# Input projection of a two-layer RWKV-7 and attention block: the work between its matmuls as queued steps, weights split a column ahead

## The chip, the cores and the metric

The kernel runs on one core of one Trainium2 chip. The metric is device time in microseconds (us) of one execution; less is better.

## What is computed

Two layers, each a token mixer and a convolutional feed-forward block, on 1024 latent and 256 context tokens of width 1024. The change touches the mixer's input projection. Cut to what matters there:

```python
mod_lat = silu(c) @ w_ada[l] + b_ada[l]          # shift, scale, gate; 6 x 1024
p = u @ w_in[l]                                  # u = x * (1 + sc1) + sh1
r, k, v, w_lo, a_lo, g_lo = split(dwconv3(p[..., :RWKV_COLS], rwkv_conv))
w_log = -softplus(-(w0 + tanh(w_lo) @ w_b)) - 0.5     # per direction
decay = exp(-exp(w_log)); a = sigmoid(a0 + a_lo @ a_b)
g = sigmoid(g_lo) @ g_b
kk = k * k_k; kk = kk / max(sqrt(sum(kk * kk)), 1e-12)    # per head of 64
k_dir = k * (1 + (a - 1) * k_a)
q = rms_norm(c_q, q_norm_g) @ w_uq; kv = rms_norm(c_kv, kv_norm_g) @ w_ukv
```

Layer 1 (the last) needs r, the queries and the gate for latent tokens only; layer 0 for all 1280.

## The kernel before

Everything is held with features on the 128 partitions and tokens along the free axis, in float32. A matmul in float32 precision is made of three fast ones: weights and inputs are split into a high and a low part (`split_w`, L259: a DMA into `raw`, a copy `whi` on ACT, a difference `wlo` on DVE), and `project` (L275, matmul in L284) adds high x high, high x low and low x high into one PSUM tile.

`in_proj` (L300) makes the projection column by column of 128 features; a column of 1280 tokens is 72 matmuls (48 of 512 tokens, 24 of 256), a latent one 48. It has two PSUM tiles for columns (tag pj) and two small ones (tag sm). Its first part makes keys and queries of the attention: columns 18 and 19 (`latent`, L327), 20, the products with w_uk and w_uv, columns 15 to 17, and `queries` (L408). Each latent's sums of squares go through a root on POOL (rs, L352) and a broadcast (`along`, L355) before its products can be scaled.

The second part makes the operands of the recurrence. `column` (L483) makes one column, and the depthwise convolution `conv` (L286) reads it from PSUM: ACT writes the middle tap (L291), DVE adds the two others (L295, L298). Columns 12 and 13 come first: inputs `lw` and `la` of the low-rank products. Then, for each of four head pairs: `key` (L501; the norm kk by block sums, L498, with Ln and Exp on ACT), `value` (L512; v less its mean, and transposes L526), r, and for each direction `operands` (L543), which takes the rank products (`lora`, L532, matmuls L538, tanh L540 on ACT), scans the decay (L550), takes exponentials E (L551, L552) and multiplies kx, rx, the keys and the rates. Direction 1 of a pair and its `bonus` come one column later, in the next pair's place. Column 14 and `gates` (L441) close the stage.

In layer 0, 40 modulations (`modulation`, L160; two weight tiles wt of 512 KB by DMA, sums L172, an evacuation ev on DVE, products L187 or L181) are spread over the 15 columns from 12 on (L488).

A scheduler (`schedule_with_timeline_sim=True`) turns the program into one queue for each engine; an engine takes its queue in order. DMAs that load weights are issued from SP's queue. A weight split is written in the program just before its column's matmuls, from a pool of 3 tiles a tag.

Of the kernel before, what the change touches and what calls it, by code (L numbers as in the profile page):

```python
# [16 lines left out]
NLAT = 1024  # L17
# [48 lines left out]
NT = 13  # L66
# [14 lines left out]
class Kern:  # L81
# [78 lines left out]
    def modulation(self, l, ch, wtile=None, pj=None):  # L160

        nc, a, M = self.nc, self.a, self.M
        cols = slice(ch * 256, (ch + 1) * 256)
        wt = []
        for k4 in range(2):
            w = (wtile or self.mod_tile)()
            nc.sync.dma_start(out=w, in_=a["w_ada"][l, ch, :, 4 * k4:4 * k4 + 4])
            wt.append(w)
        ps = M.pp.tile([128, 512], F32, name="ps", tag="sm")
        for k in range(8):  # L170
            r = 32 * (k % 4)
            nc.tensor.matmul(ps[r:r + 32, :256], M.sc[:, k, :], wt[k // 4][:, k % 4, :], start=k < 4, stop=k >= 4)  # L172
        ev = M.p.tile([128, 256], F32, name="ev", tag="ev", bufs=2)
        nc.vector.tensor_copy(ev, ps[:, :256])
        sel = self.cst[:, CO_SEL:CO_SEL + 2]
        s = ch // 4
        pt = pj.tile([128, 1536], F32, name="pt", tag="pj") if pj else M.pp.tile([128, 512], F32, name="pt", tag="sm")
        if s in (2, 5):
            mt = M.p.tile([2, 256], F32, name="mt", tag="mt", bufs=2)
            nc.sync.dma_start(out=mt, in_=a["b_ada"][l:l + 1, cols].to_broadcast([2, 256]))  # L180
            nc.tensor.matmul(pt[0:2, :256], sel, ev, start=True, stop=True)  # L181
            nc.vector.tensor_tensor(mt, pt[0:2, :256], mt, op=ALU.add)
            nc.sync.dma_start(out=self.mods[l].rearrange("r s d -> r (s d)")[:, cols], in_=mt)
            return

        for i in range(2):
            nc.tensor.matmul(pt[:, 2 * i:2 * i + 2], ev[:, i * 128:(i + 1) * 128], sel, start=True, stop=True)  # L187
        k = 2 * (ch % 4)
        dst = self.msc[l][:, s - s // 3, :, k:k + 2]
        b = bc(self.pv[l][:, None, PV_BA + 2 * ch:PV_BA + 2 * ch + 2], [128, 2, 2])  # L190
        nc.vector.scalar_tensor_tensor(dst, pt[:, 0:4].rearrange("p (k r) -> p r k", r=2), float(s in (1, 4)), b,
                                       op0=ALU.add, op1=ALU.add)
# [38 lines left out]
    def first_u(self, p, pp, pj):  # L231
# [17 lines left out]
        for i, ch in enumerate((0, 4, 1, 5, 2, 6, 3, 7)):  # L249
            self.modulation(0, ch, lambda: spare.pop(0)(), pj)  # L250
# [8 lines left out]
    def split_w(self, src, n, p):  # L259
# [3 lines left out]
        for o in range(0, n, 512):  # L263
            m = min(512, n - o)
            raw = p.tile([128, 512], F32, name="raw", tag="raw")
# [34 lines left out]
    def in_proj(self, l, up):  # L300
        tc, nc, a = self.tc, self.nc, self.a
        need_ctx = l < DEPTH - 1
        pv = self.pv[l]
        with ExitStack() as st:
# [3 lines left out]
            todo = []  # L308
            if l == 0:
                self.alloc_u(up)  # L310
                self.mod_setup(st, 2, sm)
                todo = [(0, ch) for ch in range(8, 24)] + [(1, ch) for ch in range(24)]

            def col(j, segs):
                w = self.split_w(a["w_in"][l, j], D, wp)
# [4 lines left out]
            with tc.tile_pool(name=f"iq{l}", bufs=1, reuse_waits="tile") as p:  # L320
# [3 lines left out]
                if l == 0:  # L324
                    self.first_u(p, sm, pj)

# [1001 lines left out]
```

## Time and profile before

| | us |
|---|---|
| median of 3 runs | 4700.81 (4693.97 to 4705.19) |
| profiled execution | 4693.84 |
| its span | 4692.1 |
| mean granted TensorE clock | 0.928 |
| PE, DVE, ACT, POOL busy | 4161.5, 2733.6, 1679.0, 548.8 |

The profile is of one execution. Engines: PE is TensorE's matmuls, PEld its weight loads, DVE VectorE, ACT ScalarE, POOL GpSimd, SP SyncE. A busy time counts instructions at work; matmuls are pipelined, so PE's busy time is partly overlap. PEclk is the granted clock as a share of full speed. A row of a wait names who waited, at which line, for whose result at which line.

In this execution layer 0's projection stage lies at 42 to 752 us and layer 1's at 2549 to 3136. The convolutions of the four key columns start at 309.92, 401.99, 506.15 and 611.72 us, and at 2771.38, 2833.96, 2927.88 and 3022.35. The first attention matmuls start at 751.91 and 3136.22.

### The profile page before, as it was taken

The page shows a single profiled execution, that of the slowest core. Times are in us where ns is not written, and L with a number is a line of the kernel's source. Part 1 is how long each engine was busy: PE and PEld are TensorE (multiplying, and loading weights), DVE is VectorE, ACT ScalarE, POOL GpSimd, SP SyncE. Part 2 cuts the span into 40 slices and gives each one's busy share as a digit, 9 for nine tenths or more (in the row PEclk, how much of TensorE's full clock was granted, in tenths as well). Part 3 has the DMA queues.
Part 4 walks back from the last instruction along what each step waited for, and adds up shares of the span by engine and source line. Part 5 has one row for each costly group of instructions (what it writes and reads, how often), then busy time and mean ns, then how long its engine had stood idle before and what let it go on. Part 6 is the DMA issues. An engine that isn't in the chain of part 4 may idle for free. (4 is left out here: it accounts for less than half of the span.)

```text
span 4692.1 us, 72915 instructions
## 1 busy us (share of the span) xinstructions
PE 4161.5 (89%) x29598; PEld 3295.4 (70%) x29598; DVE 2733.6 (58%) x4939; ACT 1679.0 (36%) x2996; POOL 548.8 (12%) x498
## 2 busy tenths in 40 slices
PE   7987777888988899999998987768889878999998
PEld 6865545777766688888886764446777656888887
DVE  3234446888885635445446224468888857555556
ACT  3213334454554432212224224354444544222222
POOL 1000000111222300000004000001111224100002
PEclk9988887999998999999998998869898989999999
DMA  4334554222323311111112222242222333111111
GB/s 170 109 132 146 163 181 144 72 71 72 88 72 124 101 36 37 45 32 39 43 39 99 85 74 97 81 143 69 65 74 74 74 117 132 61 50 45 45 52 66
DMA packets 425697, 401.36 MB, mean 86 GB/s; under 512 B 243472, under 2 KB 329936, under 8 KB 425360
## 3 DMA queue, kind: packets, MB, share of 16 engines
q1 hardware_dynamic: 425360, 396.69, 27.4%
q8 instruction: 233, 3.82, 0.3%
q14 instruction: 104, 0.85, 0.1%
HBM read 285.85 MB, written 110.72 MB: 85 GB/s over the span
## 5 line engine op out<-in xcount | busy, mean ns | idle before, releaser
L1139 PE MATMUL up<-u,hi 128*128 128x512 f32 (+1 forms) x3520 | 1012.9, 369 | 5.8 <-ACT hi L1130 5.8
L1139 PEld LDWEIGHTS up<-u,hi 128*128 128x128 f32 x3520 | 643.7, 189 | 121.4 <-ACT hi L1130 6.5
L1139 PE MATMUL up<-u,lo 128*128 128x512 f32 (+1 forms) x1760 | 648.8, 369 | 0.2
L284 PE MATMUL pj<-u,whi 128*128 128x512 f32 (+1 forms) x1888 | 567.1, 385 | 62.4 <-DVE o L298 35.3
L1186 DVE TENSOR_TENSOR acc<-dn,acc 128x512 f32<-128x512 f32 x340 | 233.4, 689 | 432.2 <-PE dn L1180 432.1
L284 PEld LDWEIGHTS pj<-u,whi 128*128 128x128 f32 x1888 | 351.2, 198 | 162.5 <-issue 58.4
L284 PE MATMUL pj<-u,wlo 128*128 128x512 f32 (+1 forms) x944 | 357.2, 379 | 22.1 <-DVE wlo L270 22.1
L1139 PEld LDWEIGHTS up<-u,lo 128*128 128x128 f32 x1760 | 332.4, 189 | 59.1 <-DVE lo L1132 1.5
L945 PE MATMUL sp<-ka,qa 96*128 96x512 f32 (+1 forms) x1200 | 315.0, 395 | 30.9 <-ACT P L958 21.5
L1180 PE MATMUL dn<-hi,fh 128*128 128x512 f32 x792 | 311.3, 393 | 8.2 <-DVE acc L1186 4.0
L1130 ACT ACTIVATE hi<-raw 128x512 fp32r<-128x512 f32 x176 | 110.3, 630 | 566.7 <-PE up L1139 563.3
L1180 PE MATMUL dn<-lo,fh 128*128 128x512 f32 x792 | 309.8, 391 | 0.0
L1180 PE MATMUL dn<-hi,fl 128*128 128x512 f32 x792 | 305.8, 390 | 0.0
L958 ACT ACTIVATE P<-sp,mx 128x512 f32<-128x512 f32 (+1 forms) x400 | 239.8, 606 | 178.4 <-DVE mx L955 125.6
L987 PE MATMUL av<-pT,va 128*64 128x128 f32 x2624 | 235.1, 303 | 52.2 <-DVE pT L982 28.2
L945 PEld LDWEIGHTS sp<-ka,qa 96*128 96x128 f32 x1200 | 213.6, 203 | 79.4 <-ACT P L958 29.8
L946 DVE TENSOR_REDUCE mx<-sp 128x1 f32<-128x512 f32 (+1 forms) x400 | 228.3, 586 | 43.1 <-PE sp L945 40.6
L270 DVE TENSOR_TENSOR wlo<-raw,whi 128x512 fp32r<-128x512 f32 (+2 forms) x110 | 71.5, 654 | 294.0 <-ACT whi L268 288.8
L977 PE MATMUL tp<-cst,P 128*128 128x128 f32 x1312 | 234.1, 301 | 5.7 <-ACT P L958 2.6
L284 PEld LDWEIGHTS pj<-u,wlo 128*128 128x128 f32 x944 | 185.4, 196 | 63.9 <-DVE wlo L270 25.4
L987 PEld LDWEIGHTS av<-pT,va 128*64 128x64 f32 x2624 | 153.4, 147 | 107.3 <-DVE pT L982 34.6
L1132 DVE TENSOR_TENSOR lo<-raw,hi 128x512 fp32r<-128x512 f32 x176 | 125.2, 714 | 175.8 <-ACT hi L1130 163.4
(254 smaller groups left out, 7227.2 us busy)
## 6 DMA issues: line engine op xcount, KB each, us to landing
wt<-in_w_ada_dram SPq DMA_DIRECT2D x96, 512.0 KB
raw<-in_w_up_dram SPq DMA_DIRECT2D x176, 256.0 KB
raw<-in_w_down_dram SPq DMA_DIRECT2D x88, 256.0 KB
raw<-in_w_in_dram SPq DMA_DIRECT2D x84, 256.0 KB
bkD<-lt SPq DMA_DIRECT2D x32, 640.0 KB
BK<-bkD SPq DMA_DIRECT2D x320, 64.0 KB
KR<-kkD SPq DMA_DIRECT2D x152, 128.0 KB
vtD<-vt SPq DMA_DIRECT2D x16, 640.0 KB
```

The lines of the kernel that those rows point to most:

```text
L270: nc.vector.tensor_tensor(lo[:, :m], raw[:, :m], hi[:, :m], op=ALU.subtract)
L284: nc.tensor.matmul(ps[:, o:o + n], ww, u[k][s], start=k == 0 and j == 0, stop=k == nk - 1 and j == 2)
L945: nc.tensor.matmul(sp[:, o - b0:o - b0 + n], q[:, qq, e], A.k[e][:, kk, o:o + n], start=m == 0, stop=m == 2)
L946: nc.vector.tensor_reduce(mx[:, i:i + 1], sp[:, :w], axis=AX.X, op=ALU.min)
L958: nc.scalar.activation(P[:, o:o + w], sp[:, :w], AF.Exp, bias=mn, scale=-1.0, accum_out=mx[:, 4 + i:5 + i])
L977: nc.tensor.transpose(tp[:, b, e], Ps[e][:, o:o + 128], self.ident)
L987: nc.tensor.matmul(av[half[e], 0:128], A.v[:, k0 // 128 + kt, half[e]], pT[:, b, e], start=kt == 0, stop=kt == nkt - 1)
L1130: nc.scalar.activation(hi, raw, AF.Copy)
L1132: nc.vector.tensor_tensor(lo, raw, hi, op=ALU.subtract)
L1139: nc.tensor.matmul(ps[:, so:so + sn], ww, uu[k][s], start=k == 0 and m == 0, stop=k == 7 and m == 2)
L1180: nc.tensor.matmul(ps, x[:, t * 128:(t + 1) * 128], w, start=m == 0, stop=m == 3 * len(js) - 1)
L1186: nc.vector.tensor_tensor(dst, ps, dst, op=ALU.add)
```

## The change

- `project` runs queued steps: after every 4 of its 8 k-tiles it pops an even share of `self.queue`.
- A list `ws` holds the weights in the order of use, and `weights()` splits one further ahead before it hands one out; pools of 4 (raw 3).
- `modulation` returns loads, sums and results. All 40 are queued in the keys' and queries' part, 8 steps a column or product.
- Columns 12 and 13 stand between the queries' latents and their products; latent sums and the root are steps.
- In a pair the columns come as k, r, v (in the last pair 14 ahead of v), and `key`, `value`, `ranks`, `operands`, `bonus` and `bonus2` return lists of steps that are woven and run within the next columns. The last pair's rest goes between the gate's four products.
- Two rope products move from POOL to DVE, the gate's scale from POOL to ACT. Temporary tiles: 12 of tag t and 5 of tag s in place of 13.

```diff
-NT = 13
+NT = 12
+NS = 5
...
+        wt, evs = [], []
+        def loads():
+            for k4 in range(2):
+                w = (wtile or self.mod_tile)()
+                nc.sync.dma_start(out=w, in_=a["w_ada"][l, ch, :, 4 * k4:4 * k4 + 4])
+                wt.append(w)
+        def sums():
+            ps = M.pp.tile([128, 512], F32, name="ps", tag="sm")
+            for k in range(8):
+                r = 32 * (k % 4)
+                nc.tensor.matmul(ps[r:r + 32, :256], M.sc[:, k, :], wt[k // 4][:, k % 4, :], start=k < 4, stop=k >= 4)
+            ev = M.p.tile([128, 256], F32, name="ev", tag="ev", bufs=2)
+            nc.vector.tensor_copy(ev, ps[:, :256])
+            evs.append(ev)
...
+        def results():
+            ev = evs[0]
...
+        return loads, sums, results
...
-            raw = p.tile([128, 512], F32, name="raw", tag="raw")
+            raw = p.tile([128, 512], F32, name="raw", tag="raw", bufs=3)
...
+        gaps = sum(-(-nk // 4) if SEGS[s][1] > 256 else 1 for s in segs)
         for s in segs:
             o, n = SEGS[s]
             for k in range(nk):
                 wh, wl = [x[:, (k % 4) * 128:(k % 4 + 1) * 128] for x in w[k // 4]]
                 for j, (ww, u) in enumerate(((wh, uh), (wh, ul), (wl, uh))):
                     nc.tensor.matmul(ps[:, o:o + n], ww, u[k][s], start=k == 0 and j == 0, stop=k == nk - 1 and j == 2)
+                if k == nk - 1 or (k % 4 == 3 and n > 256):
+                    self.between(-(-len(self.queue) // gaps))
+                    gaps -= 1
+    def between(self, n):
+        for _ in range(min(n, len(self.queue))):
+            self.queue.pop(0)()
...
-            wp = st.enter_context(tc.tile_pool(name=f"iw{l}", bufs=3, side="right", reuse_waits="tile"))
+            wp = st.enter_context(tc.tile_pool(name=f"iw{l}", bufs=4, side="right", reuse_waits="tile"))
...
+            ws = [a["w_in"][l, j] for j in (18, 19, 20)] + [a["w_uk"][l, j] for j in range(NP)] + [a["w_uv"][l]]
+            ws += [a["w_in"][l, j] for j in (15, 16, 17, 12, 13)] + [a["w_uq"][l, j] for j in range(6)]
+            for q in range(NP):
+                ws += [a["w_in"][l, j] for j in ([4 + q, q, 14, 8 + q] if q == NP - 1 else [4 + q, q, 8 + q])]
+            ws.append(a["g_b"][l])
+            ahead = []
+            def weights():
+                for _ in range(2 - len(ahead)):
+                    if ws:
+                        w = ws.pop(0)
+                        ahead.append(self.split_w(w, w.shape[-1], wp))
+                return ahead.pop(0)
...
+                todo = [(0, ch) for ch in range(8, 24)] + [(1, ch) for ch in range(24)] if l == 0 else []
+                mods = [self.modulation(*m) for m in todo]
+                steps = [m[0] for m in mods[:2]]
+                for i, m in enumerate(mods):
+                    steps += [m[1]] + [x[0] for x in mods[i + 2:i + 3]] + [m[2]]
+                share = -(-len(steps) // 17)
+                def some():
+                    queue.extend(steps[:share])
+                    del steps[:share]
...
+                        def sums(i=i, sq=sq):
+                            ssp = sm.tile([128, 512], F32, name="ssp", tag="sm")
+                            for t in range(nt):
+                                nc.tensor.matmul(ssp[:, t:t + 1], sq[:, t * 128:(t + 1) * 128], self.cst[:, CO_ONE:CO_ONE + 1],
+                                                 start=True, stop=True)
+                            if i:
+                                nc.vector.tensor_tensor(ss[:, :nt], ss[:, :nt], ssp[:, :nt], op=ALU.add)
+                            else:
+                                nc.vector.tensor_copy(ss[:, :nt], ssp[:, :nt])
...
+                for j, (x, f) in enumerate(((lw, AF.Tanh), (la, AF.Copy))):
+                    some()
+                    ps = col(ALL)
+                    o = tmp("o")
+                    self.conv(o, ps, PV_CONV + 3 * (12 + j), pv, True)
+                    nc.scalar.activation(x, o, f)
+                rb = along(rs, nr, -QK_SCALE)
...
+                short = name in ("kx", "rx", "oc", "ocr", "vt")
+                return p.tile([128, NTOK], dt, name=name, tag="s" if short else "t", bufs=NS if short else NT)
...
+                ss = blocks(sq, NTOK, lambda ps, s: nc.vector.tensor_scalar(sq[:, s], ps, 1e-24, None, op0=ALU.max))
+                return ss + [lambda: nc.scalar.activation(sq, sq, AF.Ln),
+                             lambda: nc.scalar.activation(sq, sq, AF.Exp, scale=-0.5),
+                             lambda: nc.vector.scalar_tensor_tensor(sq, o, kcol, sq, op0=ALU.mult, op1=ALU.mult)]
...
+                return out[:3] + [lambda: scan(0)] + out[3:5] + [lambda: scan(NTOK // 2)] + out[5:] + [decay, keys]
...
+                return [kx, rx, lambda: stt(ta, ta, 1.0, rv(kk), op0=ALU.add, op1=ALU.mult), b2,
+                        lambda: tt(kd, kd, rv(k), op=ALU.mult), k2]
...
+            def weave(x, y):
+                r = [((i + 0.5) / len(v), j, f) for j, v in enumerate((x, y)) for i, f in enumerate(v)]
+                return [f for _, _, f in sorted(r, key=lambda e: e[:2])]
...
+            old = ps = None
+            for q in range(NP):
+                c = {}
+                if old:
+                    old["v"] = convolved(8 + q - 1, ps, True)
+                    queue += weave(operands(old, q - 1, 1) + bonus(old, q - 1), value(old, q - 1))
                 else:
-                    og = column(14, need_ctx)
-                if old:
-                    q0, k0, kk0, v0, r0, kd0 = old
-                    kb = bonus(q0, [kd0, operands(q0, 1, k0, kk0, r0)], r0, v0)
-                if q == NP:
-                    gates(og, nr)
-                    bonus2(q0, kb, v0)
-                    break
-                v = value(q)
-                if old:
-                    bonus2(q0, kb, v0)
-                r = column(q, need_ctx)
-                old = q, k, kk, v, r, operands(q, 0, k, kk, r)
+                    queue += ranks(c, q, 0)
+                ps = col(ALL)
+                c["k"] = convolved(4 + q, ps, True)
+                queue += weave(bonus2(old, q - 1) + ranks(c, q, 0), key(c, q)) if old else key(c, q)
+                ps = col(segs)
+                c["r"] = convolved(q, ps, need_ctx)
+                queue += weave(operands(c, q, 0), ranks(c, q, 1))
+                if q == NP - 1:
+                    ps = col(segs)
+                    og = convolved(14, ps, need_ctx)
+                    nc.scalar.activation(og, og, AF.Tanh, scale=0.5)
+                    nc.scalar.activation(og, og, AF.Copy, scale=0.5, bias=0.5)
+                    gh, gl = tmp("gh", F32R)[:, :nr], tmp("gl", F32R)[:, :nr]
+                    nc.scalar.activation(gh, og, AF.Copy)
+                    nc.vector.tensor_tensor(gl, og, gh, op=ALU.subtract)
+                ps = col(ALL)
+                old = c
+            old["v"] = convolved(8 + NP - 1, ps, True)
+            rest = weave(operands(old, q, 1) + bonus(old, q), value(old, q)) + bonus2(old, q)
+            w = weights()
+            parts = [[[x[:, so:so + sn] for so, sn in SEGS[:len(segs)]]] for x in (gh, gl)]
+            for i in range(NP):
+                queue += rest[:8]
+                del rest[:8]
+                ps = pj.tile([128, 1536], F32, name="pj", tag="pj")
+                wq = [[x[:, i * 128:(i + 1) * 128] for x in w[0]]]
+                self.project(ps, wq, *parts, segs)
+                g = tmp("g")
+                nc.scalar.activation(g[:, :nr], ps[:, :nr], AF.Copy)
+                nc.sync.dma_start(out=self.gD[l][i, :, :nr], in_=g[:, :nr])
+            assert not rest and not queue
```

How the queues of the engines move at three places. Lines of the changed kernel differ: L298 is `project`'s matmul, L588 the rank product, L541 the block sum, L316 and L319 the convolution's taps, L598 the scan, L178 and L197 a modulation's sums and results.

PE, layer 1, around the rank products of the second pair; before, then after (lo: rank products from lw and la; bs: block sums; pj: a column, from parts u_... of the input):

```order
L284 MATMUL pj<-u_20805,whi 128x512
L284 MATMUL pj<-u_20806,whi 128x512
L284 MATMUL pj<-u_20805,wlo 128x512
L538 MATMUL lo<-lw,wb 128x512
L538 MATMUL lo<-lw,wb 128x256
L538 MATMUL lo<-la,ab 128x512 x2
L538 MATMUL lo<-la,ab 128x256
L498 MATMUL bs<-o,cst 128x512 x2
L284 MATMUL pj<-u_20803,whi 128x512
```

```order
L298 MATMUL pj<-u_20814,whi 128x256
L298 MATMUL pj<-u_20815,whi 128x256
L298 MATMUL pj<-u_20814,wlo 128x256
L588 MATMUL lo<-lw,wb 128x512 x2
L541 MATMUL bs<-sq,cst 128x256
L588 MATMUL lo<-lw,wb 128x256
L588 MATMUL lo<-la,ab 128x512 x2
L588 MATMUL lo<-la,ab 128x256
L588 MATMUL lo<-lw,wb 128x512 x2
L588 MATMUL lo<-lw,wb 128x256
L588 MATMUL lo<-la,ab 128x512 x2
L298 MATMUL pj<-u_20810,whi 128x512
```

Before, six rank products (one direction) stand at the end of a latent column (r's); after, twelve (both directions) stand together between the end of v's column and the next k column, of which all but the last 256-wide one are shown.

DVE, layer 1, around r's convolution; before, then after (o: the convolved column, kx and lt and kd: operands of one direction, sq: kk):

```order
L516 SCALAR_TENSOR_TENSOR oc<-bs,o 128x256
L270 TENSOR_TENSOR wlo<-raw,whi 128x512
L295 SCALAR_TENSOR_TENSOR o<-pj,pv_96,o 128x1023
L270 TENSOR_TENSOR wlo<-raw,whi 128x512
L298 SCALAR_TENSOR_TENSOR o<-pj,pv_96,o 128x1023
L580 TENSOR_TENSOR kd<-bs,o 128x512 x2
L550 SCALAR_TENSOR_TENSOR lt<-rst,lt 128x640 x2
L270 TENSOR_TENSOR wlo<-raw,whi 128x512
L558 TENSOR_TENSOR kx<-sq,E_22508 128x1280
```

```order
L552 SCALAR_TENSOR_TENSOR sq<-o,pv_96,sq 128x1280
L598 SCALAR_TENSOR_TENSOR lt<-rst,lt 128x640 x2
L621 TENSOR_TENSOR kx<-sq,E_22717 128x1280
L638 SCALAR_TENSOR_TENSOR lt<-lt,sq 128x1280
L639 TENSOR_TENSOR kd<-kd,o 128x1280
L316 SCALAR_TENSOR_TENSOR o<-pj,pv_96,o 128x1023
L631 SCALAR_TENSOR_TENSOR lt<-lt 128x1280
L319 SCALAR_TENSOR_TENSOR o<-pj,pv_96,o 128x1023
L635 TENSOR_TENSOR lt<-kd,lt 128x1280
```

Before, r's convolution (L295, L298) comes ahead of the scan and the first direction's operands; after, it comes behind the scan, kx and two more products of that direction.

PE, layer 0, modulations; before (a head pair's column) and after (the keys' products):

```order
L538 MATMUL lo<-la,ab 128x512 x2
L538 MATMUL lo<-la,ab 128x256
L172 MATMUL ps<-wt,sc 32x256 x8
L187 MATMUL pt<-cst,ev 128x2 x2
L172 MATMUL ps<-wt,sc 32x256 x8
L187 MATMUL pt<-cst,ev 128x2 x2
L498 MATMUL bs<-o,cst 128x512 x2
L284 MATMUL pj<-u_111,whi 128x512
```

```order
L298 MATMUL pj<-lh,whi 128x256
L298 MATMUL pj<-ll,whi 128x256
L298 MATMUL pj<-lh,wlo 128x256
L197 MATMUL pt<-cst,ev 128x2 x2
L178 MATMUL ps<-wt,sc 32x256 x8
L298 MATMUL pj<-lh,whi 128x512
L298 MATMUL pj<-ll,whi 128x512
L298 MATMUL pj<-lh,wlo 128x512
```

Before, a modulation's sums and its results follow each other; after, one modulation's results and a later one's sums stand between column matmuls.

## Rows read from the trace of the kernel before

**Rows 1.** Windows, layer 0: stretch, length, PE PEld DVE ACT POOL busy, PEclk, DMA share, GB/s.
```profile
42.00:240.00 198.00, 183.24 (x986) 150.87 (x985) 61.13 (x96) 52.49 (x86) 14.08 (x9) 0.96 0.28 95
240.00:310.00 70.00, 50.39 (x256) 38.95 (x260) 19.45 (x28) 9.66 (x13) 6.32 (x6) 0.78 0.35 117
310.00:402.00 92.00, 85.62 (x520) 62.60 (x508) 32.25 (x53) 27.95 (x37) 0.00 (x0) 0.96 0.43 141
402.00:506.00 104.00, 80.67 (x434) 54.03 (x434) 49.57 (x62) 35.60 (x45) 0.00 (x0) 0.88 0.51 174
506.00:612.00 106.00, 81.97 (x430) 54.42 (x430) 51.20 (x67) 36.31 (x49) 0.00 (x0) 0.87 0.48 160
612.00:752.00 140.00, 102.10 (x437) 60.08 (x437) 79.29 (x91) 54.13 (x64) 2.67 (x3) 0.70 0.49 172
```

**Rows 2.** Windows of layer 1's stage, same columns.
```profile
2549.00:2705.00 156.00, 150.52 (x725) 125.19 (x726) 37.12 (x48) 33.30 (x47) 6.10 (x3) 0.94 0.23 79
2705.00:2771.00 66.00, 46.74 (x219) 37.77 (x218) 17.62 (x23) 9.56 (x12) 6.38 (x6) 0.84 0.28 91
2771.00:2834.00 63.00, 63.00 (x291) 48.33 (x290) 24.53 (x28) 27.02 (x35) 0.00 (x0) 1.00 0.23 74
2834.00:2928.00 94.00, 67.71 (x271) 45.28 (x270) 44.61 (x45) 36.79 (x49) 0.00 (x0) 0.85 0.24 85
2928.00:3022.00 94.00, 66.69 (x252) 44.52 (x252) 43.33 (x43) 35.09 (x45) 0.00 (x0) 0.81 0.25 88
3022.00:3136.00 114.00, 70.22 (x196) 40.70 (x196) 69.22 (x61) 53.06 (x65) 5.80 (x8) 0.69 0.38 134
```

**Rows 3.** Waits of PE in layer 1's stage (2540 to 3140): total us, times, longest.
```profile
PE bs L498 <- DVE o L298: 37.2, 3, 12.8
PE pj L284 <- DVE o L298: 32.8, 5, 11.7
PE lo L538 <- ACT lt L540: 14.0, 9, 3.4
PE pj L284 <- DVE wlo L270: 11.5, 1, 11.5
```

**Rows 4.** Waits of ACT in layer 1's stage, same columns.
```profile
ACT whi L268 <- PE pj L284: 149.0, 30, 13.6
ACT whi L268 <- DMA raw<-in_w_in_dram: 38.3, 5, 10.0
```

**Rows 5.** Timeline of PE in layer 1's first column: start, us, instruction.
```profile
2557.21 0.63 PE L284 MATMUL pj<-u,whi 128*128 128x512 f32 x2
2557.91 0.63 PE L284 MATMUL pj<-u,whi 128*128 128x512 f32 x2
2563.16 0.39 PE L284 MATMUL pj<-u,whi 128*128 128x256 f32 x2
2563.50 0.39 PE L284 MATMUL pj<-u,whi 128*128 128x256 f32 x2
```

**Rows 6.** Timeline of PE and DVE around the last pair's rank products, layer 1.
```profile
3045.18 1.12 PE L538 MATMUL lo<-lw,wb 64*128 64x512 f32 x2
3058.53 1.49 DVE L558 TENSOR_TENSOR kx<-sq,E 128x1280 f32<-128x1280 f32 x1 [1.81 <-ACT E L551]
```

**Rows 7.** Groups of DVE by form, layer 1's head pairs: busy, mean ns, idle before.
```profile
L295 DVE SCALAR_TENSOR_TENSOR o<-pj,pv,o 128x1023 f32<-128x1023 f32 x13 | 16.6, 1279 | 23.8 <-ACT o L291 23.8
L560 DVE SCALAR_TENSOR_TENSOR lt<-lt,sq 128x1280 f32<-128x1280 f32 x8 | 11.9, 1488 | 7.3 <-ACT kd L556 7.3
```

**Rows 8.** Groups of PE by form, layer 0's modulations (42 to 768), same columns.
```profile
L172 PE MATMUL ps<-wt,sc 128*32 128x256 f32 x640 | 57.9, 452 | 4.3 <-ACT lt L540 2.3 <-ACT vt L527 1.8 <-DMA wt<-in_w_ada_dram 0.2
L187 PE MATMUL pt<-cst,ev 128*128 128x2 f32 x96 | 16.7, 279 | 28.9 <-DVE ev L174 25.4 <-ACT lt L540 3.6
L181 PE MATMUL pt<-ev,cst 128*2 128x256 f32 x32 | 12.0, 465 | 19.2 <-DVE ev L174 16.0 <-ACT lt L540 3.2
```

**Rows 9.** The page's DMA issues.
```profile
wt<-in_w_ada_dram SPq DMA_DIRECT2D x96, 512.0 KB
```

More of the change, by code (lines that the diff above doesn't have):

```diff
@@ L163, in modulation @@
         cols = slice(ch * 256, (ch + 1) * 256)
[L164 to L192, printed above, removed]
+        wt, evs = [], []
@@ L249, in first_u @@
         for i, ch in enumerate((0, 4, 1, 5, 2, 6, 3, 7)):
-            self.modulation(0, ch, lambda: spare.pop(0)(), pj)
+            for step in self.modulation(0, ch, lambda: spare.pop(0)(), pj):
+                step()
             if i == 3:
@@ L434, in in_proj @@
-                queries()
+                ch, cl, rs = latent(3, PV_QN, segs, nr)
+                for j, (x, f) in enumerate(((lw, AF.Tanh), (la, AF.Copy))):
+                    some()
+                    ps = col(ALL)
[3 more added lines that the diff above has]
+                rb = along(rs, nr, -QK_SCALE)
+                cosT, sinT = tmp("cosT"), tmp("sinT")
+                L = slice(0, NLAT)
@@ new lines, in in_proj @@
+                nc.sync.dma_start(out=cosT[:, L], in_=a["rope"][0])
+                nc.sync.dma_start(out=sinT[:, L], in_=a["rope"][1])
+                xs = []
+                for j in range(6):
+                    w = weights()
+                    ps = pj.tile([128, 1536], F32, name="pj", tag="pj")
+                    some()
+                    self.project(ps, w, ch, cl, segs)
+                    t = times(ps, rb, nr)
+                    if j < 4:
+                        nc.sync.dma_start(out=qd[2 * j:2 * j + 2, 0:64, :nr], in_=t[:, :nr])
+                    else:
+                        xs.append(t)
@@ L480, in in_proj, with one @@
                 nc.gpsimd.memset(E[d][:, :, 0:1], 1.0)
-            made = iter(range(15))
-            def column(j, full=True):
-                n = NTOK if full else NLAT
-                ps = col(j, (0, 1, 2) if full else (0, 1))
-                i = next(made)
-                for m in todo[len(todo) * i // 15:len(todo) * (i + 1) // 15]:
-                    self.modulation(*m)
-                o = tmp("o")
-                self.conv(o, ps, PV_CONV + 3 * j, pv, full)
-                return o[:, :n]
             def blocks(x, n, use):
-                for so, sn in SEGS[:3 if n > NLAT else 2]:
+                def one(so, sn):
                     ps = sm.tile([128, 512], F32, name="bs", tag="sm")
@@ L532, in lora @@
-            def lora(w, x, bcol, q, d):
-                t = tmp("lt")
-                b = bcol + 4 * d + q
-                for so, sn in SEGS:
-                    ps = sm.tile([128, 512], F32, name="lo", tag="sm")
-                    nc.tensor.matmul(ps[:, :sn], w[half[d], q * 128:(q + 1) * 128], x[half[d], so:so + sn], start=True, stop=True)
-                    dst = t[:, NTOK - so - sn:NTOK - so] if d else t[:, so:so + sn]
-                    nc.scalar.activation(dst, ps[:, sn - 1::-1] if d else ps[:, :sn], AF.Tanh, bias=hb[:, b:b + 1], scale=0.5)
-                return t
@@ new lines, in ranks, with one, scan @@
+            def ranks(c, q, d):
+                out = []
+                for nm, w, x, bcol in (("L", wb, lw, 0), ("a", ab, la, 8)):
+                    b = bcol + 4 * d + q
+                    def one(so, sn, nm=nm, w=w, x=x, b=b):
+                        if so == 0:
+                            c[nm, d] = tmp("lt")
+                        t = c[nm, d]
+                        ps = sm.tile([128, 512], F32, name="lo", tag="sm")
+                        nc.tensor.matmul(ps[:, :sn], w[half[d], q * 128:(q + 1) * 128], x[half[d], so:so + sn], start=True, stop=True)
+                        dst = t[:, NTOK - so - sn:NTOK - so] if d else t[:, so:so + sn]
+                        nc.scalar.activation(dst, ps[:, sn - 1::-1] if d else ps[:, :sn], AF.Tanh, bias=hb[:, b:b + 1], scale=0.5)
+                    out += [lambda s=s, one=one: one(*s) for s in SEGS]
+                def scan(t):
+                    Ls = c["L", d]
+                    if t == 0:
+                        nc.scalar.activation(Ls, Ls, AF.Copy, scale=0.5, bias=0.5)
```

262 lines of the change are left out of this document (124 added, 138 removed).

## Prediction

> **What bounds the kernel now.** I read the windows first, cut at the instants that part the stage: the convolutions of the four key columns, and the first attention matmul behind the stage. [rows 1] and [rows 2] are to be read along three columns: length, PE busy, and the clock granted. The reader should see two kinds of stretch. In the keys' and queries' part (first two rows of each group) and in the first head pair (third) PE is busy nearly all the time. In the later pairs it isn't: 67.71 of 94 us and 66.69 of 94 in layer 1, 80.67 of 104 and 81.97 of 106 in layer 0, and 70.22 of 114 and 102.10 of 140 in the last stretches. The granted clock falls with it, from 1.00 in the full stretch 2771 to 2834 to 0.85, 0.81 and 0.69 (1.00 is the upper level, 2.4 GHz; a smaller mean is a stretch that stood in part at the lower one, 1.2 GHz). No other engine is full there either: DVE has 44.61 us of work in 94, ACT 36.79. So those stretches are bound by a chain of waits between engines, not by an engine.
>
> The waits say which [rows 3]. PE's matmuls of the mean of v (bs<-o) wait 37.2 us for v's convolution on DVE; the next column's matmuls wait 32.8 us for the same instruction, because it holds one of the two PSUM tiles; rank products wait 14.0 us for ACT to empty a small tile; one weight split made too late costs 11.5 us. ACT's waits [rows 4] show the splits bound to the column: 149.0 us in which a split waits until PE has freed its weight tile.
>
> How much PE work is in a pair? Busy time times granted clock gives work at the full clock: 67.71 x 0.85 = 57.6 and 66.69 x 0.81 = 54.0 [rows 2], so 56 us in layer 1. In layer 0, 80.67 x 0.88 = 71.0, less 8 modulations (priced below at 1.8 us) 14.4, is 57; with that stage's longer r column I take 59. These are the floors that the change could reach.
>
> **The change part by part.**
>
> *Modulations.* All 40 now stand in the keys' and queries' part of layer 0; before, 5 of them fell there (columns 12 and 13) and about 8 in each later pair. PE's busy time for them is 57.9 + 16.7 + 12.0 = 86.6 us [rows 8], 2.17 each; those stretches ran at about 0.85 [rows 1], so 1.8 us each at full clock. Their waits, 28.9 + 19.2 = 48 us [rows 8], 1.2 each, came from running the sums and the results back to back; in the new order a sum and a result have 16 or so column matmuls between them, so I take those at nothing, hidden by the column; if the cover fails they cost 35 x 1.2 = 42 us more. Added there: 35 x 1.8 = 63 us. The DMAs move with them: 80 loads of 512 KB [rows 9], 41 MB. The stretch before loaded 198 x 95 + 70 x 117 KB/us = 27 MB, so 68 MB in 311 us, 219 GB/s; the fastest stretch of [rows 1] had 174 at a DMA share of 0.51, so the engines hold it on average. But the loads go out on SP's queue in order, and a column's weight load can stand behind a modulation load that waits for its tile: bound, one wait of the longest kind seen, 10.0 us [rows 4], in each of a few columns. I take none and keep 30 us for the range.
>
> *Keys' and queries' part.* The gain: latent sums and the root become steps, weights come early, and the two columns 12 and 13 fill the hole where the queries waited for the root. In [rows 1] 42 to 310 is 268 us with 183.24 x 0.96 + 50.39 x 0.78 = 215 of full-clock work, in [rows 2] 222 with 181. I give back 20 us in each, half of what stands above the floor: bounds 0 and 40. Layer 0: 268 - 20 + 63 = 311, **+43**. Layer 1: **-20**. The two small rope products that move from POOL to DVE and the gate's scale on ACT are instructions of about 1.2 us beside PE work: nothing.
>
> *The later pairs.* The order shows that the rank products were not spread as the queue has them: all 12 of both directions stand in one clump behind the v column. And on DVE r's convolution now stands behind both scans, kx and two products of the first direction. So a chain remains: (a) from the k column's end PE does the r and v columns with the steps between them, 56 less the next k column's 14 and some 6 of the clump, 36 us. A full column is 48 matmuls by 0.70/3 and 24 by 0.34/3 [rows 5], 14.0; a latent one 11.2. (b) The clump's own chain: before, from the first rank product to the end of kx took 3045.18 to 3060.02, 14.8 us [rows 6]; then two products of 1.49, one more woven in and the two parts of r's convolution of 1.28 [rows 7], 7.0. (c) Only then is r's PSUM tile free for the next k column, 14.0. Sum 36 + 14.8 + 7.0 + 14.0 = 72; at a clock of 0.92 in place of 1.00 (the run's mean is 0.928) PE's 56 us become 61, so **78**. Layer 0's r column has a third part, 2.8 us, plus its block sums: **82**. Before, 94 and 94, 104 and 106. The first periods (third row of each group) have no older pair to weave: 63 becomes 56, its full-clock work without the rank products of the other direction moved behind; 92 loses 8 modulations with their waits (3.0 each, 24) and gains longer columns back: 60 to 68, I take 60. Layer 0: 302 to 60 + 82 + 82 = 224, **-78**. Layer 1: 251 to 56 + 78 + 78 = 212, **-39**.
>
> *The last stretch.* Here DVE is the floor: 69.22 of 114 us [rows 2], 79.29 of 140 with 8 modulations' evacuations [rows 1], about 77 without. Column 14 goes ahead of v, and the last pair's remaining steps lie between the small gate products, so DVE has work while PE has. What stays bare is the start, v's column and its convolution, 14 + 1.3 less what DVE still does: 15 us. So 69 + 15 = 84 and 77 + 15 = 92: **-30** and **-48**. Bounds: from the DVE floors (-45, -63) to half the gain.
>
> Beside the trace, one rule speaks against this change. Rows 2 show that the clock was granted in full only where PE had no gap (63.00 of 63 us), and at 0.81 to 0.85 where it waited between groups. The Trainium skill's page "TensorE: Matmul & The Clock Gate", section "A second HAM failure mode: psum-queue depth-cycling", says that PE pauses between groups of matmuls that cycle through PSUM make the clock swing between its levels, and that throughput falls even though single matmuls look right. The steps add such group changes, so by that rule the periods stay near their old length; by the rows, fewer waits mean a higher clock. I go by the rows and keep the other as rival B.
>
> Sum: +43 - 78 - 48 - 20 - 39 - 30 = -172. The profiled execution took 4693.84 us (span 4692.1), so **4522**. The median of the runs, 4700.81, is 7 us above; that is inside their spread, and I don't add it. Nothing behind the stage changes. About 0.2%, 9 us, is what a measurement of this kernel can tell from no change.
>
> **Rivals.**
>
> *A, PE-bound pairs.* The chain closes and periods fall to PE's work at 0.92, 61 and 64 us. For: DVE and ACT have only 45 and 37 us a pair. Against: the clump in the order, with two small PSUM tiles. Four periods save 17.5 more each, 70, and the last stretches reach DVE's floor, 24: **4428**.
>
> *B, the clock gives it back.* The waits get shorter but more, PE runs the pairs at the 0.69 to 0.81 of the late stretches, and 56 us of work becomes 69 to 81 before any wait. The four periods keep their 94 to 106 us: 398 in place of 320, +78: **4600**. For: the fall of the clock in [rows 1] and [rows 2]. Against: the first period's 1.00 with the same columns.
>
> *C, slower.* PE takes its queue in order, and every step is now an instruction that must have its operand and a free small tile when the column reaches it. A pair has 27 small tiles (12 rank products, 9 block sums, 6 groups of transposes), 216 in 8 pairs. Before, a rank product that waited for ACT lost 14.0/9 = 1.6 us [rows 3]. If each step loses that, 216 x 1.55 = 335 us: **4857**. It decides from 172/216 = 0.80 us a step on. Against: before, only 9 such waits were seen, since most tiles were free in time, and steps have column matmuls ahead of them to wait under.
>
> That the change doesn't do what it says holds in part only: the ranks' clump. Weights, modulations and columns stand as written.
>
> **Numbers.** The forecast 0.55, its own range 4480 to 4570 (30 us of loads, 40 of the start, 30 of the last stretches, not all at once). A 0.16, B 0.21, C 0.08. The range takes in A's 4428 and B's 4600 with 25 us for the modulations' waits: 4428 to 4625; outside are C and the ends of A and B. Faster by over 0.2%: all but C and a sliver of B, 0.91; same 0.02; slower 0.07.
>
> **What would show it.** In the profile after: layer 0's first k convolution 40 us later, its DMA share over 0.45 there; k to k about 80 us with PE's clock over 0.9; bs<-o no longer PE's longest wait; ACT's splits waiting for loads, not for PE; the last stretch 85 to 92. Wrong if PE's waits for small tiles sum to over 100 us, or if the clock in the pairs stays at 0.85 or less while the waits are gone.

## The result, and the profile after

The changed kernel took 4592.53 us (median of 4 runs, 4577.93 to 4594.17), the kernel before in the same comparison 4703.0 (4693.97 to 4711.5): ratio 0.9758, 95% interval 0.9731 to 0.9786. It is faster by some 110 us, inside the range of 4428 to 4625, but short of the 172 us of the sum and outside the forecast's own range of 4480 to 4570. The two profiled executions have spans of 4574.3 and 4692.1 us, 117.8 apart, so the stretches can be set against the forecast one by one.

The windows of the changed kernel, first layer 0 (cut at the start of the stage, beside columns 12 and 13, once more among the queries' products, at the four key convolutions and at the first attention matmul), then layer 1 from columns 12 and 13 on; columns as in [rows 1]:

```profile
39.00:240.00 201.00, 192.37 (x1273) 149.60 (x1271) 67.36 (x139) 50.17 (x82) 12.15 (x8) 0.95 0.58 200
240.00:312.00 72.00, 60.84 (x430) 45.97 (x430) 23.38 (x41) 10.10 (x12) 1.97 (x1) 0.94 0.57 194
312.00:387.00 75.00, 53.66 (x292) 37.99 (x290) 21.32 (x33) 11.84 (x16) 0.81 (x4) 0.84 0.35 117
387.00:431.00 44.00, 38.22 (x162) 27.35 (x162) 27.93 (x26) 22.90 (x27) 0.00 (x0) 0.90 0.19 72
431.00:519.00 88.00, 73.45 (x284) 50.52 (x285) 54.65 (x56) 36.39 (x46) 0.00 (x0) 0.83 0.31 115
519.00:597.00 78.00, 69.50 (x282) 48.44 (x280) 46.44 (x48) 36.75 (x47) 0.00 (x0) 0.85 0.32 116
597.00:692.00 95.00, 81.98 (x325) 57.88 (x323) 53.69 (x55) 47.85 (x56) 1.74 (x2) 0.82 0.38 128
...
2660.00:2737.00 77.00, 55.93 (x225) 41.39 (x224) 23.68 (x27) 16.29 (x24) 0.93 (x4) 0.84 0.24 82
2737.00:2782.00 45.00, 39.35 (x162) 28.16 (x162) 27.38 (x25) 20.88 (x24) 0.00 (x0) 0.89 0.17 67
2782.00:2859.00 77.00, 67.77 (x253) 45.42 (x254) 45.59 (x47) 35.57 (x45) 0.00 (x0) 0.87 0.33 118
2859.00:2939.00 80.00, 69.15 (x259) 46.80 (x259) 49.43 (x50) 36.13 (x46) 0.00 (x0) 0.85 0.33 115
2939.00:3025.00 86.00, 72.48 (x259) 48.04 (x258) 50.45 (x50) 45.63 (x56) 1.41 (x2) 0.82 0.39 130
```

| stretch | before | forecast | after |
|---|---|---|---|
| layer 0: start to second key convolution | 360 | 371 | 392 |
| layer 0: two periods | 104 + 106 | 82 + 82 | 88 + 78 |
| layer 0: last stretch | 140 | 92 | 95 |
| layer 0: mixer (first attention matmul to first output product) | 708 | 708 | 726 |
| layer 1: start to second key convolution | 285 | 258 | 277 |
| layer 1: two periods | 94 + 94 | 78 + 78 | 78 + 80 |
| layer 1: last stretch | 114 | 84 | 86 |

Periods and last stretches came out as forecast, within 6 us. Three places did not: the front of each layer's stage (21 and 19 us long) and layer 0's mixer (18 us). What PE waits for tells where to look, layer 0's stage first (39 to 692), then layer 1's (2504 to 3025), as in [rows 3]:

```profile
PE ps L178 <- DMA wt<-in_w_ada_dram: 26.8, 4, 9.9
PE pj L298 <- DVE o L319: 23.0, 5, 10.4
PE lo L588 <- ACT lt L590: 15.6, 10, 3.2
...
PE lo L588 <- ACT lt L590: 17.3, 9, 3.9
PE lo L588 <- DMA wb<-in_w_b_dram: 15.0, 1, 15.0
PE pj L298 <- DVE o L319: 14.9, 3, 10.9
...
PE bs L541 <- DVE o L319: 3.7, 1, 3.7
```

In layer 1 the wait for v's mean fell from 37.2 us [rows 3] to 3.7, the wait for a PSUM tile from 32.8 to 14.9, and the late split is gone. Two new waits stand there: modulation weights in layer 0, and the load of the rank weights wb in layer 1.

### The profile page after: what moved, and what is told of

It reads as the page before. It is cut to its first block, busy times and chain, and to the rows that moved or that the text cites. A ratio compares the mean times of both kernels' runs of the same rounds, so it can differ in the third digit from the quotient of the medians.

```text
span 4574.3 us, 72907 instructions
## 1 busy us (share of the span) xinstructions
PE 4139.9 (91%) x29598; PEld 3290.5 (72%) x29598; DVE 2738.4 (60%) x4943; ACT 1687.0 (37%) x3000; POOL 537.9 (12%) x492
## 4 chain that ended last, share of the span: by engine, by line
PE 53%; DVE 12%; ACT 4%; DMA 3%; issue 2%; POOL 1%; SPq 1%; POOLq 0%; DVEq 0%; ACTq 0%
PE up L1243 23%; PE dn L1284 11%; PE pj L298 6%; PE ps L1193 3%; PE sp L1049 2%; PE av L1091 2%; PE tp L1081 2%; PE g L858 2%; DVE T L900 1%; DVE mx L1050 1%; DVE tmp L899 1%; DVE pT L1086 1%; DMA raw<-in_w_o_dram 1%; ACT P L1062 1%; PE lo L588 1%
## 5 line engine op out<-in xcount | busy, mean ns | idle before, releaser
L298 PE MATMUL pj<-u,whi 128*128 128x512 f32 (+1 forms) x1888 | 564.5, 383 | 42.8 <-DVE o L319 37.9
L298 PEld LDWEIGHTS pj<-u,whi 128*128 128x128 f32 x1888 | 351.7, 198 | 140.6 <-issue 47.4
L298 PE MATMUL pj<-u,wlo 128*128 128x512 f32 (+1 forms) x944 | 361.1, 383 | 0.2 <-DVE wlo L283 0.2
L281 ACT ACTIVATE whi<-raw 128x512 fp32r<-128x512 f32 (+2 forms) x110 | 66.2, 603 | 464.5 <-PE pj L298 414.9
L298 PEld LDWEIGHTS pj<-u,wlo 128*128 128x128 f32 x944 | 185.2, 196 | 41.9 <-issue 10.5
```

## Experiments

In all comparisons below a stage runs from the first column matmul to the first attention matmul of its layer. In the changed kernel: 652.5 us in layer 0, 520.6 in layer 1.

**Is the mixer's loss the change's?** `b_bar` and `a_bar` put one line ahead of each mixer:

```diff
+            tc.strict_bb_all_engine_barrier()
             self.mixer(0, wst)
```

> The kernel before with an all-engine barrier ahead of each layer's mixer, so that the scheduler plans both mixers from an empty state. Theory 1 (the change gave back 16 us in layer 0's mixer because the scheduler ordered that untouched code anew): this kernel alone shows the price of the barriers, 5 to 30 us slower than before (4705 to 4730 us), with no other shift. Rival (the mixer's length hangs on the stage's own tail, its DMAs and the clock): same price; the two part only in the difference to the changed kernel with the same barriers.

> The changed kernel with the same two barriers. Layer 1's mixer then stands in the same order on PE, ACT and POOL as in the kernel before with barriers; layer 0's does not. Theory 1: layer 1's mixer and what follows takes the same time in both kernels with barriers, within 3 us, and the difference of the two kernels in layer 1 is that of the stage alone, about 67 us; in layer 0's mixer, ordered anew, some of the 16 us stays. Rival (the tail of the stage decides): with a drained machine both mixers take the same time in both kernels, and the difference of the totals grows from 118 to 60 + 67 = 127 us or more.

The barriers cost more than forecast: b_bar 4772.52 us (ratio 1.0136, 1.011 to 1.0162); without them stage and mixer overlap (in b_bar layer 1's stage is 49 us longer than in the kernel before, its mixer 46 shorter). a_bar took 4643.65 (0.9868, 0.9842 to 0.9894). Layer 1's mixer, in the same order in both, took 651.5 us in both, as both theories had it; its stage differs by 58.7. The spans differ by 138, 51 of it in layer 0's stage. Layer 0's mixer took 736.2 in b_bar and 706.2 in a_bar, the other way round from the pair without barriers (708 and 726), and 30 of the 138 us, which neither theory had. So the loss of 18 us isn't a fixed price of the change. Three runs whose PE, VectorE, ScalarE and SP queues are those of the changed kernel up to there say what it is: layer 0's mixer took 725.6 (a_noload), 742.1 (a_atonce) and 744.1 (a_wb). The windows of the changed kernel and of a_wb, the same 100 us of mixer:

```profile
892.00:992.00 100.00, 87.48 (x1155) 68.73 (x1155) 82.88 (x215) 51.00 (x117) 20.09 (x23) 0.84 0.29 73
```

```profile
894.00:994.00 100.00, 87.62 (x1052) 68.73 (x1050) 73.04 (x189) 47.62 (x108) 17.51 (x21) 0.74 0.27 66
```

PE is as busy but gets through 1052 matmuls in place of 1155: the granted clock was 0.74 of 2.4 GHz, not 0.84, so more of it stood at 1.2 GHz. With equal queues layer 0's mixer varies by 18 us from run to run; a difference of one profiled pair there is no evidence. The kernel before varies too: b_w4 (below) has its queues up to the end of this mixer, and took 720.7 us where the kernel before took 707.6. Since all four executions of the changed kernel lie above both, a loss stays possible.

**Rank weights early, layer 1** (`a_wb`):

```diff
+            if l == 1:
+                wb, ab = [lp.tile([128, 512], F32, name=nm) for nm in ("wb", "ab")]
...
+                if l == 1:
+                    nc.sync.dma_start(out=wb, in_=a["w_b"][l])
+                    nc.sync.dma_start(out=ab, in_=a["a_b"][l])
                 rb = along(rs, nr, -QK_SCALE)
...
```

> The changed kernel, layer 1 only: the two tiles of rank weights (wb, ab) in the pool that lives through the stage, loaded ahead of the queries' products, not in the pool that opens behind them. Theory: PE's wait of 15.0 us for wb's load was a new bound of its own; it goes, layer 1's stage falls from 520.6 to 506 to 509 us, the total by 12 to 15. Rival: the first rank products would have waited for something else at the same place (conv, small tiles), and the stage stays within 4 us.

4585.45 us (0.9738, 0.9713 to 0.9762); layer 1's stage 517.5, down 3.1: the rival. (Up to the second key convolution it gained 5.6 us, of which the first period gave back 2.4.) PE's and ACT's waits in its front (2681 to 2758) show what stood behind wb:

```profile
PE lo L593 <- ACT lt L595: 15.3, 1, 15.3
```

```profile
ACT lt L595 <- DMA qD<-tm: 6.2, 1, 6.2
```

ScalarE's first tanh waits for a query store to leave: its tile lies in the pool that opens where the queries' temporaries lay. So behind wb stood a wait for the change of pools. In the changed kernel wb's own load stood behind the last two query stores on SP's queue: they were issued from 2701.86 us on, the load at 2704.89, and PE had it at 2715.49.

**Modulation loads left out** (`a_noload`, `a_noload2`). In the first the edit asks for kept weights before any load has run, so it has no effect; it is a repeat of the changed kernel: 4585.08 us (0.9743, 0.9717 to 0.9768), stages 652.4 and 522.1, which shows how well stages repeat.

> The changed kernel without 38 of the 40 modulations' loads: all take the weights of the first in the stage (the later modulations have other values). PE, DVE and ACT work is the same. Theory 1 (the front part of layer 0 came out 18 us longer than forecast because modulation loads are late, with PE waiting 27 us for them): layer 0's stage falls by 25 to 40 us, the wait ps<-wt to under 3. Rival (the extra time is PE's work on the modulations and the lower clock): the stage falls by under 8 us, and other waits take the place of these.

```diff
         def loads():
+            if pj is None and getattr(self, 'wt0', None):
+                wt.extend(self.wt0)
+                return
             for k4 in range(2):
...
+            if pj is None:
+                self.wt0 = list(wt)
```

> The changed kernel without 38 of the 40 modulations' loads in the keys' and queries' part: all take the weights of the first one there (the modulations have other values). The run named a_noload was meant to be this, but its edit never took hold and its queues are those of the changed kernel; it serves as a repeat. Theory 1 (the front of layer 0 is longer than forecast because PE waits 27 us for modulation loads): layer 0's stage falls from 652.5 by 20 to 35 us and the wait for wt goes. Rival (the drain of the pool behind the queries sets the end of that part anyway): the stage falls by under 8 us, and the idle time moves to the first rank products and the first key column.

4571.91 us (0.9728, 0.9706 to 0.9751); layer 0's stage 632.3, down 20.2, and no wait for wt is left. From the start to the second key convolution it took 373 us, where 371 had been forecast with loads at nothing. Theory 1 holds.

**Rope products first** (`a_rope`):

```diff
-                for j in range(6):
+                for j in (4, 5, 0, 1, 2, 3):
...
+                    if j == 5:
+                        x1, x2 = xs
...
```

> The changed kernel with the two rope products of w_uq first among the six and their six VectorE instructions and two stores right behind them, so that the part ends with a plain product and its store. Theory 2 (the second part's first tiles lie where the first part's temporaries lay, and ScalarE's first tanh waits for the last query stores; the rope's tail of 6 x 1.2 us and its stores end last): both stages fall, by 6 to 12 us each, the totals by 12 to 24. Rival (the first key column would wait at the same place for its weights, whose loads of 10 us stand last on SP's queue): under 3 us a layer.

Slower than the changed kernel: 4622.03 us (0.9832, 0.9812 to 0.9852); stages 656.0 and 534.0, up 3.5 and 13.4: neither theory had that. In layer 1 PE (2690 to 2815) and SP's queue (2690 to 2745) now wait

```profile
PE lo L588 <- DMA wb<-in_w_b_dram: 33.1, 1, 33.1
```

```profile
SPq L522 <- DMA qD<-tm: 13.1, 1, 13.1
```

PE waits twice as long for wb, because SP holds wb's load for 13.1 us until a query store has left: the change of pools itself. The rope's tail is out of the way there, and the last store is a plain product's. That product was done at 2702.5 us, but SP, which stood at a weight load from 2707.0 to 2719.0, issued the store only at 2719.14.

**Where steps and splits are written** (`a_atonce`):

```diff
         nk = len(uh)
+        self.between(len(self.queue))
...
-                    self.between(-(-len(self.queue) // gaps))
```

> The changed kernel with each column's queued steps written all ahead of its matmuls, not between them; weights ahead, the order of columns and all else stay. Theory (what the steps bring is work between matmuls: PE waits under them): periods go back toward 90 to 100 us, the stage of layer 1 from 520.6 to 560 or more, layer 0's modulations bring back their 1.2 us of waits each, 40 us. Rival (the scheduler, which sorts each queue by its own plan, does the interleaving, and weights ahead bring the gain): stages within 10 us of the changed kernel's.

4598.15 us (0.9766, 0.9742 to 0.9791), stages 652.9 and 522.4. Its queues are, instruction by instruction, those of the changed kernel on PE, VectorE, ScalarE and SP, so it is one more repeat: the rival, as far as the steps go. The scheduler sorts by its own plan. The same holds on PE, VectorE and ScalarE for weights split without the written lead (only SP's DMAs stand otherwise), by a comparison of the two programs and not by a run. So neither the place of a step within its column nor the written lead moves anything by itself. That the steps come a column later, and in another order, was not undone here.

**Weight tiles** (`a_w3`, `b_w4`):

```diff
-                for _ in range(2 - len(ahead)):
+                for _ in range(1 - len(ahead)):
...
-            wp = st.enter_context(tc.tile_pool(name=f"iw{l}", bufs=4, side="right", reuse_waits="tile"))
+            wp = st.enter_context(tc.tile_pool(name=f"iw{l}", bufs=3, side="right", reuse_waits="tile"))
```

> The changed kernel with weights as before: one column's at a time, pools of 3 tiles. (The scheduler's queues showed that the written lead alone moves nothing on PE, VectorE and ScalarE: without it they are the same word for word; so are all queues with the steps written ahead of each column, which the run a_atonce therefore repeats.) Theory W (the fourth weight tile is what lets PE go on with the next column while a convolution runs): k to k in layer 1 goes back from 77.6 and 79.8 to 90 us or more, its stage from 520.6 to 550 to 580. Rival O (the order in which PSUM tiles, small tiles and columns are handed out makes the gain): stage of layer 1 within 15 us of 520.6.

> The kernel before with four weight tiles a tag in layer 1 (three raw); layer 0, where a fourth does not fit, stays as it is. Theory W: layer 1's periods fall from 94 to 78 to 84, its stage from 587.3 to 540 to 560, the wait of splits for PE shrinks. Rival O: the stage stays within 10 us of 587.3, since PE waits for v's convolution and for the PSUM tile, not for weights.

a_w3: 4586.27 us (0.9758, 0.974 to 0.9775), layer 1's stage 522.3, layer 0's 663.1. b_w4: 4684.29 us (0.9966, 0.9953 to 0.9979), layer 1's stage 584.6 against 587.3. (b_w4 is the kernel before with four tiles in layer 1.) Rival O: in layer 1's stage a fourth weight tile is worth no more than repeats differ by (520.6 to 522.4 in the changed kernel; in layer 0's stage, where b_w4 has the queues of the kernel before, 707.2 against 710.3). In layer 0's stage it is worth 11; that this comes of modulation loads on the same SP queue is not shown. b_w4's 0.3% is a difference of medians; its profiled execution is only 2.9 us shorter, so the rest can't be looked for there. In b_w4 (2540 to 3130) splits make PE wait 3.4 us in place of 24.1, and the time goes to the next wait:

```profile
PE pj L284 <- DVE o L298: 51.1, 6, 18.3
PE bs L498 <- DVE o L298: 37.6, 3, 13.2
```

What remains, by exclusion, for the gain in the periods is the new order of columns, of the steps a column later, and of the tiles they use (PSUM, small tiles, temporaries). It was not undone alone, so this is argued and not shown.

**Modulations moved alone** (`b_mods`, the kernel before, `mods()` making three modulations):

```diff
                         ps = col(j, segs)
+                        mods()
...
                     self.project(ps, w, ch, cl, (0, 1, 2))
+                    mods()
```

> The kernel before with the 40 modulations written in the keys' and queries' part, three behind each of 14 columns or products, sums and results back to back as before; nothing else moved. Theory (my sum: the front pays 35 x 1.8 = 63 us and 42 for uncovered waits, the later pairs lose 3.0 for each of 35 modulations, 105): the start of the first key convolution moves from 309.9 to 365 to 415, layer 0's k to k falls to 92 to 96 as in layer 1, the stage as a whole changes by less than 15 us. Rival (the loads, 41 MB in 270 us, come late as in the changed kernel): the front pays over 110 us and the stage grows by 15 or more.

Slower: 4728.67 us (1.0061, 1.004 to 1.0081), layer 0's stage 728.2 against 710.3. The first key convolution moved from 309.92 to 388.0, its periods became 95.1 and 95.6, about layer 1's 94. So the front paid 78 us, in the span of the theory and not the rival's 110, and the stage grew by 18, which only the rival had:

```profile
PE ps L172 <- DMA wt<-in_w_ada_dram: 30.4, 5, 9.5
```

Moving the modulations, with sums and results back to back as before, is a loss of its own; columns and pairs must pay for it.

**The clump** (`a_ranks0`):

```diff
-                    queue += weave(operands(old, q - 1, 1) + bonus(old, q - 1), value(old, q - 1))
+                    queue += weave(operands(old, q - 1, 1) + bonus(old, q - 1), ranks(c, q, 0)) + value(old, q - 1)
...
-                queue += weave(bonus2(old, q - 1) + ranks(c, q, 0), key(c, q)) if old else key(c, q)
+                queue += key(c, q) + bonus2(old, q - 1) if old else key(c, q)
```

> The changed kernel with another order of the steps: a pair's first-direction rank products come in its key column (woven with the older pair's operands), ahead of the older pair's mean of v and transposes; key's block sums come ahead of the older pair's bonus. In the queue of PE the clump of twelve rank products is gone. Theory (the clump behind v's column, held back by the two small PSUM tiles that are handed out in program order, makes the 78 us of a period): four periods fall from 77.6 to 88 to 62 to 72 us, the total by 30 to 60. Rival (the chain from v's convolution through the next pair, or VectorE's queue, holds the period): periods within 4 us of what they were, or longer, since kx then waits with a full set of temporaries.

4563.55 us (0.9706, 0.9687 to 0.9725), a median 29 us below the changed kernel's; the profiled executions are 14 apart. Key convolutions of layer 1:

```profile
2779.80 1.31 ACT L312 ACTIVATE o<-pj,pv 128x1280 f32<-128x1280 f32 x1
...
2849.27 1.31 ACT L312 ACTIVATE o<-pj,pv 128x1280 f32<-128x1280 f32 x1
...
2920.32 1.31 ACT L312 ACTIVATE o<-pj,pv 128x1280 f32<-128x1280 f32 x1
```

Periods of 69.5 and 71.0 in place of 77.6 and 79.8; layer 0's are 76.1 and 75.4. The first period grew by 7 to 9 us, and layer 0's last stretch by 4, so of 31 us in the periods the stages kept 9. The theory's mechanism holds, in size only for layer 1; the key's block sums moved in the same edit, so their share isn't known.

**A kernel that beats both** (`a_poolq`: a_ranks0, a_wb, and one more edit):

```diff
-                nc.sync.dma_start(out=w, in_=a["w_ada"][l, ch, :, 4 * k4:4 * k4 + 4])
+                (nc.sync if pj else nc.gpsimd).dma_start(out=w, in_=a["w_ada"][l, ch, :, 4 * k4:4 * k4 + 4])
```

> A kernel meant to beat the changed one: the order of steps of the run a_ranks0, the early rank weights of a_wb in layer 1, and in layer 0 the modulations' loads of the keys' and queries' part issued from POOL's queue in place of SP's, so that a load that waits for its tile holds up no weight and no store. Theory (modulation loads cost 20 us, as a_noload2 showed, because they stand in one queue with everything else): layer 0's stage falls from 650.9 (a_ranks0) to 632 to 642. Rival (they are late because their tiles come free late, whatever the queue; or POOL's own work on descriptors is slower): 648 or more. Layer 1's stage, 513.4 in a_ranks0, falls by 3 to 10 if wb's load was a wait there, else stays.

4538.58 us (0.9656, 0.9634 to 0.9678), the fastest here. Layer 0's stage is 637.6, 13 below a_ranks0; layer 1's 505.0, 8 below, in its front. POOL's waits (40 to 400) show the loads that now wait where no weight load and no store stands behind them, and PE's (240 to 390) what came in place of wt:

```profile
POOL wt L170 <- PE ps L178: 195.3, 37, 19.0
```

```profile
PE pt L197 <- DVE ev L180: 13.4, 1, 13.4
PE pj L298 <- DVE o L319: 10.5, 1, 10.5
```

The Trainium skill's page "DMA: Bandwidth & Descriptors", section "Issuing engine by pattern", calls SP's and ScalarE's hardware path generally faster than GpSimd's. No run here times one load by both; the stage got 13 us faster on GpSimd's path, so the line a load stands in weighed more than the path.

## Why the prediction was right, and where it fell short

- **The number** is right in part by luck. The forecast's own range, 4480 to 4570, was missed; the stated one holds 4592.53 because it takes in rival B's 4600, and B's longer periods did not come.
- **The bound** (a chain of waits, not an engine) was right: the waits named [rows 3] went, from 37.2 to 3.7 and from 32.8 to 14.9 us, with the same matmuls on PE.
- **The later pairs**: "so **78**", and "**82**" for layer 0, met 77.6, 79.8, 77.8 and 88.0. The clump, read from the order, is a link of the chain: a_ranks0 took it away and layer 1's periods fell by 8 to 9 us. r's late convolution was not tested. One term in it was wrong: the clock was put at 0.92, and the rows after show 0.83 to 0.87, no higher than the 0.81 to 0.88 of before [rows 1, 2]. With that clock the same chain would be 72 + 56 / 0.85 - 56 = 82 in layer 1, so some part of it was put about 3 us too long; which, no run tells. That the two errors cancel is luck. (By its own terms, 72 + 61 - 56, the 78 is 77; and the 24 us for rival A's last stretches are 30 by the DVE floors given for them. Neither changes the outcome.)
- **The last stretches**: 84 and 92 forecast, 86.2 and 94.7 measured.
- **Modulations**: the failed step is "I take none and keep 30 us for the range". The loads cost 20 us (a_noload2), of the 21 that layer 0's front missed by; another queue alone gave 13 back (a_poolq against a_ranks0). The average of 219 GB/s said nothing on them: a load waits for its tile, at the head of SP's queue (changed kernel, 240 to 390):

```profile
SPq L170 <- PE ps L178: 28.4, 11, 7.7
```

  The term put at nothing beside it, results hidden under column matmuls, was right: PE's waits for ev, 25.4 + 16.0 us over the stage before [rows 8], are 1.8 after.
- **Keys' and queries' part, layer 1**: the failed step is "I give back 20 us in each, half of what stands above the floor", with 7 more in the first period. It gave 8 of 27. The idle time ahead of the first key convolution only changed its name: 66 - 46.7 = 19 us before [rows 2], 11.5 of it the late split, and 77 - 55.9 = 21 after, 15.0 of it for wb, behind the last query stores (a_wb, a_rope); halving an idle time without naming its cause was no estimate. With a_ranks0's order, early rank weights did bring 8 us there.
- **"Nothing behind the stage changes"**: the code didn't, its order did, and the profiled pair differs by 18 us in layer 0's mixer. Runs with equal queues vary by 13 and by 18 us there, so it can't be put down to the change; it can't be excluded either.
- **Rivals.** A (PE-bound pairs) did not come, nor C: waits of rank products for ScalarE in layer 1 are 17.3 us, against 14.0 in [rows 3]. B's fall of the clock is there, but not its longer periods.
- **The signs** of "What would show it" came out mixed. Met: the DMA share of layer 0's front (0.58 and 0.57), the periods, bs<-o no longer PE's longest wait, and, within 3 us, the last stretches. Missed: layer 0's first key convolution came 78 us later, not 40 (front and first period shifted against each other, so the table above takes them together); the clock stayed under 0.9; and ACT's splits still wait for PE in layer 1 (2504 to 3025), 140.7 us against 149.0 [rows 4]:

```profile
ACT whi L281 <- PE pj L298: 140.7, 36, 13.6
ACT whi L281 <- DMA raw<-in_w_in_dram: 38.5, 5, 10.0
```

  The sign of being wrong, a clock of 0.85 or less in the pairs while the waits are gone, was touched: 0.83 and 0.85, 0.87 and 0.85. The periods fell all the same.
- The reason given in the change's name, steps between matmuls, brought nothing by its place within a column (a_atonce); my account of the gain did not rest on it but did not see it either.

## What to carry to other kernels

Where a scheduler sorts the queues, compare the queues of a variant with those of the original before reading anything into its source: two of this change's edits moved no instruction on PE, VectorE or ScalarE, while another order of the same steps (a_ranks0) moved the periods by 8 us each in layer 1. Give a load that must wait for its tile a queue in which nothing else stands behind it. And ask of every boundary between pools what the first instructions behind it wait for.

## What was not expected of the hardware

Runs with the same queues through layer 0's mixer differed there by 18 us (725.6 to 744.1), with the granted clock of one 100-us stretch at 0.74 against 0.84, while the same runs' projection stages agreed within 1.2 us (651.7 to 652.9). In the kernel before two executions with the same queues differed there by 13 us (707.6 and 720.7).
